# A fixed TensorE order in the mixing stage, and state products in 64-column form

## The chip, the cores and the metric

The kernel runs on one core of a Trainium2 chip. The metric is the device time of one execution in microseconds. Three runs of the kernel before took 3265.79, 3265.83 and 3274.77 us, median 3265.83. One more execution was profiled; it took 3262.19 us, and all rows below are from it.

## The reference, cut to what matters

One layer of a decoder on 2,048 tokens of 1,024 channels, in float32. Half of the channels go through an RWKV-7 recurrence, half through dilated attention; the mixture is projected and normalised, then follow a mixture of 32 experts, a gated embedding and a second normalisation.

```python
proj = h @ w_in                                  # r,k,v for 8 rwkv heads, q,k,v for 8 attention heads
# rwkv, per head, over the tokens (state is 64 x 64):
sa    = state @ a_t
state = state * w_t + outer(sa, b_t) + outer(v_t, k_t)
y_t   = state @ r_t
# attention: three patterns (window, step) = (128,1), (512,4), (2048,16), each with a bias and a softmax,
# then one softmax over the three log-sums weighs the three results
x = layer_norm(ALPHA * x + concat(y_rwkv, y_att) @ w_o)
x = layer_norm(ALPHA * x + experts(x) + sigmoid(x @ G) * (p @ P))
```

## The kernel before, in words

The kernel runs its stages one after the other: project (inputs to r, k, v, q and what the recurrence needs), mixers (recurrence and attention), mix_out (normalising the recurrence's heads, product with w_o, first normalisation, router), ple, experts, finish. The change is in mixers, from about 860 to 1800 us of the profile.

The recurrence is worked in chunks of 128 tokens. The eight heads form four pairs u, and a pair lies on the 128 partitions, one head on 64. For a pair and two chunks (q = 0 to 7, c = 0, 1) three generators do the work. rwkv_front (L652) makes triangular products (triangles, L650), sends their diagonal blocks through DRAM twice, inverts them on VectorE (L691, L692) and leaves U. rwkv_inverse (L706) turns U into the inverse of the whole triangle with ten small products and copies, and ends with WF (L800). rwkv_state (L803) makes the products that belong to a chunk (L822 to L865: RB, MK, MJ, E, Q, the transposed v in vt) and then goes from chunk to chunk (L867 to L890). This last loop has the two products of the change:

- the next state. pn is MK x vt plus E x st over the whole 128 by 128 (L875, L877), though a state has only the two diagonal blocks of 64 by 64, one for each head. MK and E hold both heads, and of pn only the diagonal blocks are read: ScalarE scales the upper one (L880), VectorE the lower one (L882), into the other of two state tiles. The blocks off the diagonal of a state tile stay at the zeros that L527 wrote.
- the output. py is vt x MJ for each head on its own 64 rows (L886), plus st x Q as one product over 128 rows (L888). ScalarE copies it out (L890).

In the first chunk there is no st, in the last no next state: 60 new states and 64 outputs over four pairs and 16 chunks.

attn_streams (L975) gives three streams that share the blocks of attention, 16 to a pass, 12 passes. A block is logits (L1066 or L1069), bias and minimum (L1079, L1082), exponential (L1085), transposes (L1091), a copy (L1095, L1097) and the product with the values (L1105), copied out by VectorE (L1117 to L1121). When the three patterns of two heads are done, combine (L1131, L1140) weighs them by way of DRAM (L1213, L1160).

All these are generators. Before each piece of work they yield an engine and a cost, such as _pe(448) or _act(64). weave (L117) is the planner: plain code that keeps one clock for each engine and picks among the streams the one that can start first, with 100 ns between two steps of a stream (LATENCY, L65), and among those within SLACK of it the one first in the list, states first. The order of the picks is the order of the program text. The Tile framework then orders the instructions of each engine by a time model of its own, so that an instruction whose operands are not there in that model is passed by others. Where a with block calls manual_schedule for an engine, that engine's instructions keep the order of the text. project (L219), mix_out (L1420) and the stages after it have such blocks for TensorE; mixers has none.

Of the kernel before, what the change touches and what calls it, by code (L numbers as in the profile page):

```python
# [12 lines left out]
AF = mybir.ActivationFunctionType  # L13
# [5 lines left out]
P = 128  # L19
# [43 lines left out]
FRONTS = 2  # L63
# [55 lines left out]
def _act(n):  # L119
    return "ACT", 190 + 0.56 * n  # L120


def _dve(n):
    return "DVE", 60 + 1.06 * n
# [6 lines left out]
def _pe(ns):  # L131
    return "PE", ns


def _wait(ns):
    return "DMA", ns
# [31 lines left out]
class K:  # L168
# [634 lines left out]
    def rwkv_state(self, i, u, q, pp):  # L803

        nc, kp = self.nc, self.rk_
        mm = nc.tensor.matmul
        ps = lambda: self.rps[i].tile([P, BT], F32, name=f"ps{i}", tag=f"ps{i}")
        T = lambda name, shape, bufs=1: kp.tile(shape, F32, name=f"{name}{i}", tag=f"{name}{i}", bufs=bufs)
        RB = T("RB", [P, 2, 2, 192])
        H = [slice(0, 64), slice(64, 128)]  # L810
        col = [slice(c * P, (c + 1) * P) for c in range(2)]
        while "v" not in pp:
            yield None
        rt, v = ([pp[m][:, cs] for cs in col] for m in ("rt", "v"))
        bk = [pp["bk"][:, c] for c in range(2)]
        MJ, MK = T("MJ", [P, 2, 2, P]), T("MK", [P, 2, P])
        yield _pe(950)
        prs = [ps().rearrange("p (c k s) -> p c k s", c=2, k=2) for _ in range(2)]
        for c in range(2):
            for m in range(2):  # L820
                for h in range(2):
                    mm(prs[h][:, c, m], bk[c][H[h], m], rt[c][H[h]], start=True, stop=True)  # L822
        for h, pr in enumerate(prs):
            yield _dve(2 * P)
            nc.vector.tensor_tensor(out=RB[:, h, :, 0:P], in0=pr[:, :, 0, :], in1=self.c("upi").unsqueeze(1).to_broadcast([P, 2, P]), op=ALU.mult)
            yield _dve(2 * P)
            nc.vector.tensor_tensor(out=MJ[:, h], in0=pr[:, :, 1, :], in1=self.c("upi").unsqueeze(1).to_broadcast([P, 2, P]), op=ALU.mult)
        vt = T("vt", [P, 2, P])
        for m in range(2):
            yield _pe(430 - 215 * m)  # L830
            pt = ps().rearrange("p (k s) -> p k s", s=P)
            for j in range(2 - m):
                for c in range(2):
                    nc.tensor.transpose(pt[:, 2 * j + c], v[c] if m else bk[c][:, j], self.c("eye"))
            yield _act((4 - 2 * m) * P)
            if m:
                nc.scalar.copy(vt, pt[:, 0:2])
            else:
                nc.scalar.copy(RB[:, :, :, P:192], pt[:, 0:2].rearrange("p c (h k) -> p h c k", h=2))
                nc.scalar.copy(MK, pt[:, 2:4])  # L840
        while "WF" not in pp:
            yield None
        WF = pp["WF"]
        pm = []
        for h in range(2):
            yield _pe(660)
            pm.append(ps()[:, 0:384].rearrange("p (c s) -> p c s", s=192))
            for c in range(2):
                mm(pm[h][:, c], WF[:, h, c, 64:192], RB[:, h, c], start=True, stop=True)
        for h in range(2):  # L850
            yield _dve(384)
            nc.vector.tensor_tensor(out=MJ[:, h], in0=pm[h][:, :, 0:P], in1=MJ[:, h], op=ALU.add)
            nc.vector.tensor_tensor(out=MK[:, :, H[h]], in0=pm[h][:, :, P:192], in1=MK[:, :, H[h]], op=ALU.add)
        yield _pe(700)
        pq = ps()[:, 0:384].rearrange("p (c s) -> p c s", s=192)
        for c in range(2):
            for h in range(2):
                mm(pq[H[h], c], WF[:, h, c, 0:64], RB[:, h, c], start=True, stop=True)
        yield _dve(256)
        E = self.E[i]  # L860
        for h in range(2):
            nc.vector.tensor_tensor(out=E[H[h], :, H[h]], in0=pq[H[h], :, P:192], in1=self.c("eye2")[H[h]].unsqueeze(1).to_broadcast([64, 2, 64]), op=ALU.add)
        yield _dve(256)
        Q = T("Q", [P, 2, P])
        nc.vector.tensor_tensor(out=Q, in0=pq[:, :, 0:P], in1=pp["rt"].rearrange("p (c s) -> p c s", s=P), op=ALU.add)  # L865
        yt = T("yt", [P, 2 * P])
        for c in range(2):  # L867
            first = q == 0 and c == 0
            last = q == 7 and c == 1
            st, after = (self.state[u][(c + n) % 2] for n in range(2))  # L870
            if not last:
                yield _pe(224 if first else 448)
                pn = ps()[:, 0:P]

                mm(pn, MK[:, c], vt[:, c], start=True, stop=first)  # L875
                if not first:
                    mm(pn, E[:, c], st, start=False, stop=True)  # L877
                yield _act(64)
                rho = self.rho[:, u, q + c, 1 - c:2 - c]
                nc.scalar.activation(after[H[0], H[0]], pn[H[0], H[0]], AF.Copy, scale=rho[H[0]])  # L880
                yield _dve(64)
                nc.vector.tensor_scalar_mul(after[H[1], H[1]], pn[H[1], H[1]], rho[H[1]])  # L882
            yield _pe(640)
            py = ps()[:, 0:P]
            for h in range(2):
                mm(py[H[h]], vt[:, c, H[h]], MJ[:, h, c], start=True, stop=first)  # L886
            if not first:
                mm(py, st, Q[:, c], start=False, stop=True)  # L888
            yield _act(128)
            nc.scalar.copy(yt[:, col[c]], py)  # L890
        nc.sync.dma_start(self.y[u * P:(u + 1) * P, q * 2 * P:(q + 1) * 2 * P], yt)
        pp["done"] = True

    def mixers(self, attention=True):

        self.y = self.scratch("y", (D, S))
        rounds = [(q, u) for q in range(8) for u in (0, 2)]
        pps = [[{}, {}] for _ in rounds]

        def load(n):  # L900
            q, u = rounds[n]
            for i in range(2):
                self.rwkv_load(u + i, q, pps[n][i])

        begun = {}

        def fronts(s):
            for n in range(s, len(rounds), FRONTS):
                if n in begun:
                    yield from begun[n]  # L910
                    continue
                while n >= ROUNDS and not all("done" in pp for pp in pps[n - ROUNDS]):
                    yield None
                load(n)
                yield _wait(2500)
                yield from self.rwkv_front(n, pps[n], pps[n - 1])

        def inverses(i):
            for n in range(len(rounds)):
                yield from self.rwkv_inverse(i, pps[n][i])  # L920

        def states(i):
            for n, (q, u) in enumerate(rounds):
                yield from self.rwkv_state(i, u + i, q, pps[n][i])
                self.steps[0] += 1

        with ExitStack() as es:
            att = []
            self.rwkv_setup(es)
            self.busy = False  # L930

            with self.tc.high_priority():
                for n in range(FRONTS):
                    load(n)
                    begun[n] = self.rwkv_front(n, pps[n], pps[n - 1])
                    while next(begun[n], None) is not None:
                        pass
            if attention:
                self.attn_open(es)
                att = self.attn_streams()  # L940
            self.steps = [0, 0]

            def late():

                return range(4 + FRONTS, 8 + FRONTS) if self.steps[1] < (self.steps[0] + HEAD) * PACE else (4 + FRONTS,)

            weave([states(0), states(1), inverses(0), inverses(1), *(fronts(s) for s in range(FRONTS)), *att], late)


    def attn_bias(self, tile, bank):  # L950
# [1042 lines left out]
```

## Time and profile before

| | before |
|---|---|
| median of 3 runs | 3265.83 us |
| profiled execution | 3262.19 us |
| its span | 3260.4 us |
| TensorE (PE) busy | 2938.1 us, 90% |
| VectorE (DVE) busy | 2118.0 us, 65% |
| ScalarE (ACT) busy | 1529.3 us, 47% |
| GpSimd (POOL) busy | 675.4 us, 21% |
| mean granted TensorE clock | 0.934 |

PE is the matmuls, PEld the weight loads that run beside them. A row's form is partitions*columns of the stationary operand, then the moving one. A matmul's row lasts until its result is out, longer than the time to the next one's start, so work is counted from start to start. "<-" names what an engine waited for.

### The profile page before, as it was taken

The page shows a single profiled execution, that of the slowest core. Times are in us where ns is not written, and L with a number is a line of the kernel's source. Part 1 is how long each engine was busy: PE and PEld are TensorE (multiplying, and loading weights), DVE is VectorE, ACT ScalarE, POOL GpSimd, SP SyncE. Part 2 cuts the span into 40 slices and gives each one's busy share as a digit, 9 for nine tenths or more (in the row PEclk, how much of TensorE's full clock was granted, in tenths as well). Part 3 has the DMA queues.
Part 4 walks back from the last instruction along what each step waited for, and adds up shares of the span by engine and source line. Part 5 has one row for each costly group of instructions (what it writes and reads, how often), then busy time and mean ns, then how long its engine had stood idle before and what let it go on. Part 6 is the DMA issues. An engine that isn't in the chain of part 4 may idle for free. (4 is left out here: it accounts for less than half of the span.)

```text
span 3260.4 us, 49197 instructions
## 1 busy us (share of the span) xinstructions
PE 2938.1 (90%) x16686; PEld 2343.0 (72%) x16687; DVE 2118.0 (65%) x4730; ACT 1529.3 (47%) x3650; POOL 675.4 (21%) x682
## 2 busy tenths in 40 slices
PE   7989888999798999998998799899999999998880
PEld 6666777777676777777786577788777777776660
DVE  4997333786654766655757688653577777766756
ACT  3434212554444544543543333311477777765642
POOL 0442000344100211111202122223011111112216
PEclk9999999999898988998897999999999999999985
DMA  5213433788615335234214453243599999987846
GB/s 172 74 59 99 107 81 80 215 273 267 139 55 127 94 74 129 72 95 104 75 31 130 144 183 123 97 138 89 181 298 322 326 301 324 315 296 220 293 129 209
DMA packets 364061, 533.04 MB, mean 163 GB/s; under 512 B 92376, under 2 KB 204640, under 8 KB 363792
## 3 DMA queue, kind: packets, MB, share of 16 engines
q1 hardware_dynamic: 330144, 459.09, 44.1%
q0 software_dynamic: 14496, 45.93, 6.0%
q10 hardware_dynamic: 19168, 24.86, 3.1%
q8 instruction: 133, 2.18, 0.3%
q14 instruction: 120, 0.98, 0.1%
HBM read 402.27 MB, written 128.06 MB: 163 GB/s over the span
## 5 line engine op out<-in xcount | busy, mean ns | idle before, releaser
L1708 DVE TENSOR_TENSOR wl<-raw,wh 128x512 fp32r<-128x512 f32 x768 | 478.3, 681 | 88.4 <-ACT wh L1707 87.7
L1707 ACT CAST wh<-raw 128x512 fp32r<-128x512 f32 x768 | 417.3, 620 | 13.2 <-DMA raw<-in_w_up_dram 12.1
L198 PE MATMUL ps<-xh,wh 128*128 128x512 f32 x640 | 262.6, 410 | 1.1 <-ACT xh L322 1.0
L199 PE MATMUL ps<-xl,wh 128*128 128x512 f32 x640 | 258.7, 404 | 1.2 <-DVE xl L323 1.2
L200 PE MATMUL ps<-xh,wl 128*128 128x512 f32 x640 | 258.2, 403 | 0.0
L1085 ACT ACTIVATE pe<-pe,ms 128x256 f32<-128x256 f32 (+1 forms) x384 | 174.8, 457 | 144.0 <-DVE ms L1082 133.0
L1837 POOL DMA_INDIRECT acc<-ysb,ix x48 | 95.8, 1996 | 623.0 <-ACT ysb L1836 403.0
L198 PE MATMUL pe<-wh,XX 128*128 128x512 f32 x480 | 199.8, 416 | 3.8 <-ACT wh L1707 3.8
L199 PE MATMUL pe<-wl,XX 128*128 128x512 f32 x480 | 192.0, 400 | 2.6 <-DVE wl L1708 2.6
L200 PE MATMUL pe<-wh,XX 128*128 128x512 f32 x480 | 190.9, 398 | 0.0
L198 PEld LDWEIGHTS ps<-xh,wh 128*128 128x128 f32 x640 | 124.7, 195 | 34.6 <-issue 2.6
L199 PEld LDWEIGHTS ps<-xl,wh 128*128 128x128 f32 x640 | 124.7, 195 | 30.1 <-DVE xl L323 2.4
L200 PEld LDWEIGHTS ps<-xh,wl 128*128 128x128 f32 x640 | 124.1, 194 | 29.5
L1091 PE MATMUL pl<-eye,pe 128*128 128x128 f32 x600 | 126.3, 299 | 10.7 <-ACT pe L1085 9.6
L1066 PE MATMUL pl<-KK,Q 128*128 128x256 f32 x432 | 115.4, 393 | 15.6 <-DMA KK<-ks 8.0
L198 PE MATMUL pb<-gh,XH 128*128 128x512 f32 x320 | 126.1, 394 | 0.0
L199 PE MATMUL pb<-gl,XH 128*128 128x512 f32 x320 | 125.2, 391 | 0.0
L1752 PE MATMUL pe<-wh,XX 128*128 128x512 f32 x288 | 120.1, 417 | 5.4 <-ACT wh L1707 5.4
L200 PE MATMUL pb<-gh,XL 128*128 128x512 f32 x320 | 124.9, 390 | 0.0
L1105 PE MATMUL po<-pe,V 128*64 128x128 f32 x1200 | 119.4, 300 | 3.6 <-DVE O L1117 3.2
L1753 PE MATMUL pe<-wl,XX 128*128 128x512 f32 x288 | 118.8, 413 | 2.9 <-DVE wl L1708 2.9
L1082 DVE CUSTOM_DVE_ANT_0 pe<-pl,bias 128x256 f32<-128x256 f32 x216 | 82.6, 418 | 59.7 <-PE pl L1066 37.4
(418 smaller groups left out, 7627.5 us busy)
## 6 DMA issues: line engine op xcount, KB each, us to landing
raw<-in_w_gate_dram SPq DMA_DIRECT2D x128, 512.0 KB
raw<-in_w_up_dram SPq DMA_DIRECT2D x128, 512.0 KB
raw<-in_w_down_dram SPq DMA_DIRECT2D x128, 512.0 KB
pk<-pk SPq DMA_DIRECT2D x32, 512.0 KB
pk_t<-pk SPq DMA_DIRECT2D x32, 512.0 KB
KK<-ks SPq DMA_DIRECT2D x64, 256.0 KB
wr<-in_w_in_dram SPq DMA_DIRECT2D x48, 256.0 KB
rkk<-rkk SPq DMA_DIRECT2D x32, 384.0 KB
```

Source lines behind the costliest of these rows:

```text
L198: mm(out, lh, rh, start=first, stop=False)
L199: mm(out, lh, rl, start=False, stop=False)
L200: mm(out, ll, rh, start=False, stop=last)
L1066: mm(pl[:, h], q, toks(KK[:, m, h], n, prev, 2), start=m == 0, stop=m == 1)
L1085: nc.scalar.activation(pe[:, h, w], pe[:, h, w], AF.Exp, bias=m_[h], scale=-1.0, accum_out=s_[h])
L1091: nc.tensor.transpose(pt[:, h, b], pe[:, h, b * P:(b + 1) * P], self.c("eye"))
L1105: mm(o[h * 64:(h + 1) * 64, j], vb[:, h * 64:(h + 1) * 64], tt[:, h, b], start=b == kb[0], stop=b == 1)
L1707: nc.scalar.copy(wh[:, c], raw[:, c])
L1708: nc.vector.tensor_tensor(out=wl[:, c], in0=raw[:, c], in1=wh.bitcast(F32)[:, c], op=ALU.subtract)
L1752: mm(ps, L[:, 0:P], wh, start=first, stop=False)
L1753: mm(ps, L[:, 0:P], wl, start=False, stop=last)
L1837: nc.gpsimd.indirect_dma_start(out=self.acc, out_offset=bass.IndirectOffsetOnAxis(ap=ix[0:r, e, b:b + 1], axis=0), in_=ysb[0:r], in_offset ...
```

## The change

In rwkv_state each product is made for the two heads apart, with 64 columns of the stationary operand each: pn shrinks to 64 columns and holds one head's state in each half of the partitions; the output's product with the state is two half products. The costs that are told to the planner are changed. In mixers, the call of weave stands in a manual_schedule block for TensorE.

```diff
             if not last:
-                yield _pe(224 if first else 448)
-                pn = ps()[:, 0:P]
-
-                mm(pn, MK[:, c], vt[:, c], start=True, stop=first)
+                yield _pe(110 if first else 220)
+                pn = ps()[:, 0:64]
+
+                for h in range(2):
+                    mm(pn[H[h]], MK[:, c, H[h]], vt[:, c, H[h]], start=True, stop=first)
                 if not first:
-                    mm(pn, E[:, c], st, start=False, stop=True)
+                    for h in range(2):
+                        mm(pn[H[h]], E[:, c, H[h]], st[:, H[h]], start=False, stop=True)
                 yield _act(64)
                 rho = self.rho[:, u, q + c, 1 - c:2 - c]
-                nc.scalar.activation(after[H[0], H[0]], pn[H[0], H[0]], AF.Copy, scale=rho[H[0]])
+                nc.scalar.activation(after[H[0], H[0]], pn[H[0]], AF.Copy, scale=rho[H[0]])
                 yield _dve(64)
-                nc.vector.tensor_scalar_mul(after[H[1], H[1]], pn[H[1], H[1]], rho[H[1]])
-            yield _pe(640)
+                nc.vector.tensor_scalar_mul(after[H[1], H[1]], pn[H[1]], rho[H[1]])
+            yield _pe(220 if first else 440)
             py = ps()[:, 0:P]
             for h in range(2):
                 mm(py[H[h]], vt[:, c, H[h]], MJ[:, h, c], start=True, stop=first)
             if not first:
-                mm(py, st, Q[:, c], start=False, stop=True)
+                for h in range(2):
+                    mm(py[H[h]], st[:, H[h]], Q[:, c], start=False, stop=True)
...
-            weave([states(0), states(1), inverses(0), inverses(1), *(fronts(s) for s in range(FRONTS)), *att], late)
+            with self.tc.manual_schedule(engines={mybir.EngineType.PE}):
+                weave([states(0), states(1), inverses(0), inverses(1), *(fronts(s) for s in range(FRONTS)), *att], late)
```

## Rows read from the trace of the kernel before

**Rows 1.** The page: busy time of the engines, and TensorE's granted clock in 40 slices

```profile
PE 2938.1 (90%) x16686; PEld 2343.0 (72%) x16687; DVE 2118.0 (65%) x4730; ACT 1529.3 (47%) x3650; POOL 675.4 (21%) x682
PEclk9999999999898988998897999999999999999985
```

**Rows 2.** Busy time by stretch; the columns stand in its first line

```profile
core 0: us, PE busy (x) PEld busy (x) DVE busy (x) ACT busy (x) POOL busy (x), PEclk, DMA share, GB/s
900.00:1800.00 900.00, 848.73 (x6702) 684.86 (x6701) 552.25 (x1929) 422.39 (x1426) 142.24 (x215) 0.91 0.36 90
1700.00:1800.00 100.00, 85.55 (x612) 68.96 (x608) 71.21 (x154) 38.13 (x96) 26.95 (x24) 0.78 0.43 113
1717.60:1815.00 97.40, 72.34 (x430) 56.66 (x428) 65.78 (x138) 32.91 (x79) 23.64 (x15) 0.72 0.56 158
```

**Rows 3.** TensorE's waits, 900 to 1800 us: us in total, times, longest

```profile
PE ps L858 <- DVE AW L721: 14.6, 2, 9.2
PE ps L877 <- DVE E L862: 8.6, 3, 7.4
PE pl L1066 <- DMA KK<-ks: 7.3, 4, 3.0
```

**Rows 4.** TensorE's timeline, one chunk: start us, us, engine, line, tiles, form, count

```profile
1445.61 0.71 PE L1091 MATMUL pl<-eye,pe 128*128 128x128 f32 x5
1446.15 0.39 PE L875 MATMUL ps<-vt,MK 128*128 128x128 f32 x2
1446.38 0.39 PE L877 MATMUL ps<-S,E 128*128 128x128 f32 x2
1446.69 0.44 PE L886 MATMUL ps<-MJ,vt 128*64 128x128 f32 x4
1447.06 0.49 PE L888 MATMUL ps<-Q,S 128*128 128x128 f32 x2
1447.48 0.71 PE L858 MATMUL ps<-RB,WF 128*64 128x192 f32 x6
```

**Rows 5.** TensorE's timeline, 1309 to 1311.4 us, products and one weight load

```profile
1308.98 0.60 PE L834 MATMUL ps<-eye,pk_t 128*128 128x128 f32 x4
1309.51 0.68 PE L788 MATMUL ps<-t,X 64*64 64x64 f32 x8
1310.12 0.33 PE L1091 MATMUL pl<-eye,pe 128*128 128x128 f32 x1
1310.29 0.60 PE L834 MATMUL ps<-eye,pk_t 128*128 128x128 f32 x4
1310.82 0.66 PE L1105 MATMUL po<-pe,V 128*64 128x128 f32 x8
1311.40 0.44 PE L834 MATMUL ps<-eye,v_t 128*128 128x128 f32 x2
...
1310.81 0.42 PEld L1105 LDWEIGHTS po<-pe,V 128*64 128x64 f32 x8 [0.17 <-issue]
```

**Rows 6.** Groups by line, 900 to 1800 us: busy us, mean ns, idle before

```profile
L1085 ACT ACTIVATE pe<-pe,ms 128x256 f32<-128x256 f32 (+1 forms) x341 | 154.7, 455 | 122.7 <-DVE ms L1082 114.5 <-PE ps L650 2.9 <-DMA KK<-ks 2.5
L1082 DVE CUSTOM_DVE_ANT_0 pe<-pl,bias 128x256 f32<-128x256 f32 x186 | 71.2, 419 | 58.3 <-PE pl L1066 36.5 <-PE po L1105 20.1 <-ACT vt L837 1.1
L1085 ACT ACTIVATION_READ_ACCUMULATOR pe<-pe,ms 128x1 f32 x341 | 64.6, 189 | 0.0
...
L875 PE MATMUL ps<-vt,MK 128*128 128x128 f32 x120 | 27.5, 313 | 0.7 <-ACT AW L728 0.4 <-DVE MK L853 0.3
```

**Rows 7.** Timelines at the stage's end

```profile
1714.70 0.59 PE L756 MATMUL ps<-U,AB 32*32 32x32 f32 x16
1715.22 0.44 PE L834 MATMUL ps<-eye,v_t 128*128 128x128 f32 x2
1716.97 0.66 PE L1105 MATMUL po<-pe,V 128*64 128x128 f32 x8 [0.28 <-ACT pe L1095]
...
1742.16 1.27 POOL L1213 TENSOR_TENSOR O<-O,O 128x512 f32<-128x512 f32 x1 [8.52 <-DMA O<-fac]
...
1748.10 0.69 DVE L1160 TENSOR_TENSOR O<-O,O 128x512 f32<-128x512 f32 x1
...
1798.00 0.47 PE L888 MATMUL ps<-Q,S 128*128 128x128 f32 x2
1810.08 0.80 PE L198 MATMUL pa<-woh,YH 128*128 128x512 f32 x1 [8.38 <-ACT YH L1335]
```

## The prediction

> **What bounds the kernel now.** I read four views in this order: the page's shares and slices, the busy time by stretches, the waits of TensorE, and the timeline of TensorE in the mixing stage. The page says that TensorE (PE) is busy for 90% of the span, VectorE (DVE) for 65% [rows 1]. The change touches only the mixing stage. Between 900 and 1800 us, nearly all of that stage, PE is busy for 848.7 of 900 us and DVE for 552.3 [rows 2], so PE bounds the stage: work taken from PE shortens it, and so does each wait at the head of its queue that goes. The waits add up to 900 - 848.7 = 51.3 us; the largest are 14.6 us for DVE before L858 and 8.6 us for DVE before L877 [rows 3].
>
> The timeline shows what PE's time is made of. A float32 product stands there as two passes (L875 has 120 rows [rows 6] for 60 products). Full-array passes of 128 columns follow each other at 0.11 us: L834 and L1091 do so, and so do L875 and L877 [rows 4, 5]. Three things matter for the change.
> - Half-array passes (128*64), issued for the two column halves, run side by side: eight L1105 passes take 1310.82 to 1311.40, 0.58 us [rows 5], that is four pairs of 0.11 and 0.14 besides.
> - That rest is the price of a change of array shape. L834's four passes take 0.53 us before a 64*64 product follows, where 4 x 0.11 = 0.44 would do [rows 5]: 0.09 to leave a shape. Entering costs about 0.05 more (0.14 - 0.09).
> - 64*64 passes of 64 columns on one quadrant come at (1310.12 - 1309.51 - 0.14)/8 = 0.06 us [rows 5].
>
> Going through this timeline from 900 to 1800 us, I count 939 places where a matmul has another array shape than the one before it; rows 4 and 5 hold some of them.
>
> At the stage's end the last attention product runs at 1716.97, the last state product at 1798.00, and the next stage only gets going after a wait of 8.4 us before 1810.08 [rows 7]. Of the 97.4 us from 1717.6 to 1815 PE is busy for 72.3, at a granted clock of 0.72 [rows 2]. That is a mean of the two levels, 2.4 and 1.2 GHz; PE had been waiting there for one chain after the other.
>
> **Part 1, the state products in 64 columns.** New state (L875, L877): four full passes of 128 columns, 4 x 0.11 = 0.448 us, become eight half-array passes of 64 columns. If the two halves run side by side as L1105's do, that is four pairs of 0.058, 0.23 us: 0.216 us saved in each of 56 products and half of that in the 4 first ones, 12.5 us. No row shows a 128*64 pass with 64 columns, so the bounds: not side by side, 8 x 0.058 = 0.46, 1 us lost; at the spacing of the smallest passes, L756's sixteen in 0.52 us [rows 7], four pairs of 0.032, about 18 us saved. I take 12.5, since the nearest row (L1105) shows pairs.
>
> Output (L886, L888): two pairs and two full passes, 0.22 + 0.22 = 0.44, become four pairs, 0.44: nothing. The measured stretch is longer, L886 at 1446.69 to L858 at 1447.48, 0.79 against L1105's 0.58 [rows 4, 5], because the shape changes inside it. That change goes, but the new state, now half-array as well, gets one at its own border. The planner's list (below) has 797 changes with the old shapes and 799 with the new, so this is no gain of its own. The copies L880 and L882 read 64 columns before and after: nothing. What the smaller products free is PE's own time; late next is the same ACT or DVE copy.
>
> The Trainium skill ("TensorE: Matmul & The Clock Gate", section "The mechanism") speaks against this part: it says that a weight load overlaps a running matmul only where the row groups differ, and both halves use all 128 rows here. This trace disagrees: L1105's eight weight loads lie within 0.42 us, under matmuls that take 0.66 [rows 5]. What the rule would give here is worked out as the last rival.
>
> **Part 2, PE's order.** The planner (weave) is plain host code that goes by its own costs. Written out for the kernel before, it makes 1,262 PE steps. In that order the array shape changes 797 times, because a step's products stay together; in the trace, steps are cut up and mixed (L834 stands twice with L788 and L1091 between [rows 5]). With 139 changes fewer at 0.14 us: 19.5 us. Bounds: 0, if the new costs reorder the steps into as many changes, and 28, if each costs 0.2 as on entering the full array (L888's two passes take 1447.06 to 1447.48, 0.42 for 0.22 of work [rows 4]).
>
> **Part 3, waits.** From now on a step whose operand is late holds all of PE. Behind a late state product stand attention's logits, transposes and value products of three streams, and behind those DVE (L1082) and ACT (L1085, L1095), which have nothing else to do for these streams. Today's order was settled instruction by instruction, with work passing by whatever was not ready: it runs attention up to some 650 matmuls ahead of the planner's order and leaves the state products to the end. How far the planner can be trusted: it counts 0.48 us for an exponential of 256 columns, the rows show 0.455 and 0.189 for its sum, 0.64 together [rows 6]; 0.33 for L1082, the row shows 0.419 [rows 6]. It is also too short for PE: 596 us in all where the stage's PE is busy for about 850 [rows 2]. Both sides stretch by about 1.3 to 1.4, so what it put between two dependent steps still roughly covers their hand-over. Bounds for the waits: down to 14 us, which leaves of 51.3 only what lies after 1700 us (85.6 of 100 busy [rows 2]); up to 110, about twice today's, or one more wait of 0.05 us at each of 1,262 steps. By the planner's own clock PE idles 9.5% until its last state product, which on this stage's 817 us of work left (848.7 less 32) would be 86 us. I take 62, the middle of the two bounds, 11 more than now.
>
> SP's and POOL's queues are not edited, but what they wait for comes in another order: loads of keys and of rwkv operands are issued when PE has read the old ones. Their rows are short today, 7.3 us for L1066 behind the key loads [rows 3]; they are inside the bounds above.
>
> **Part 4, the end.** In the planner's list the last state product is step 1,186, and the 76 after it are attention's. So the end turns round: today the rwkv chain is last, and of the 97.4 us after 1717.6 some 45 are lost (72.3 busy at a clock of 0.72 are 52 us of work at the full one [rows 2]). Afterwards attention is last, then its weighting: 25 us from the last product to the first multiplication (1716.97 to 1742.16 [rows 7]), 6 more to the first finished slice (L1160 at 1748.10), 12 until a result is back in the next stage, as today from the last state product to the first unbroken run (1798.00 to 1810.08 [rows 7]): 43, and a little where three streams are alone. I take no difference, with 25 us either way.
>
> **The sum.** -12.5 (part 1) - 19.5 (part 2) + 11 (part 3) + 0 (part 4) = -21 us. The profiled execution took 3262.2 us (span 3260.4 and 1.8 around it), which gives 3241. The median of the runs shown is 3265.8, 3.6 above it; on that scale, which the times below use too, 3245.
>
> **The rivals.**
> - A, the order is better than I allow. Waits fall to 14 us: -12.5 - 19.5 - 37 = -69, 3197. For it: PE has much parallel work, and the state chain, late today, would be in step. Against it: PE already has only 5.7% idle.
> - B, slower: PE blocks at the head of its queue. The mechanism is part 3's, all along the stage, where a state or inverse step waits for DVE (L862, L853, L750) with attention behind it. It decides once the waits exceed 51 + 32 = 83 us. At 110 us, with the clock's half level a little more often (a mean of 0.90 for 0.91 [rows 2], 10 us), it is -32 + 59 + 10 = +37: 3303. For it: DVE is 61% busy in the stage [rows 2], the planner's hand-overs of 0.1 us and costs are short, and its own idle share gives 86. Against it: PE's own steps stretch as much.
> - C, no difference. The new passes don't pair, and the order brings as many waits as it saves changes: +1 - 19.5 + 20 = about 0, 3266.
> - D, slower: the halves' weight loads wait for the running passes. Eight loads of 0.053 (L1105's 0.42 [rows 5]) and eight passes of 0.058 are 0.89 for a new state (+0.44); with passes of 0.11 they are 1.30 for an output (+0.51 on 0.79); over 60 products +57 us, with the rest of the sum (-19.5 + 11) 3314. L1105 stands against it. It is the rule named in part 1 that would make it so.
>
> **Chances.** Forecast 0.46, A 0.12, B 0.27, C 0.12, D 0.03. A measurement of this kernel can tell about 0.3%, 10 us, from nothing. The forecast's own range is 3220 to 3262, most of it faster by more than 10 us (0.40), a little within (0.06). With A this gives faster 0.52; same is 0.12 and 0.06, 0.18; slower 0.30. The range over all cases, from A's time to short of B's farther end, is 3200 to 3305.
>
> **What would show it.** The row of L875 with 240 passes of 64 columns and pairs 0.06 us apart: part 1; at 0.11 a pair, it brings nothing. Fewer than 850 changes of shape between 900 us and the stage's end: part 2. PE's idle time in the stage: 62 us for the forecast, over 83 for B. The last attention product after the last state product: part 4. The prediction is wrong if the stage's end moves by more than 45 us, or if time moves in stages after it that the change leaves alone.

## The result and the profile after

The kernel after takes 3381.67 us (median of 4 runs, 3377.93 to 3387.09); the kernel before took 3265.81 beside it. The ratio is 1.0351, 95% interval 1.0328 to 1.0374: slower by 3.5%, where 0.6% faster was forecast, and outside the forecast range. The profiled execution took 3378.72 us, 116.5 more than that of before.

All of it lies in the mixing stage. The first product of the next stage's output bank (pn at L1322, now L1326) starts at 1931.47 us instead of 1815.06, 116.4 later. The change moves all later line numbers: by 1 to 3 in the state loop, by 4 in the attention and the next stage (L1105 is L1109).

The page after, first its busy times, then the granted clock of the 40 slices:

```profile
PE 2895.4 (86%) x17038; PEld 2294.3 (68%) x17039; DVE 2119.1 (63%) x4730; ACT 1535.3 (45%) x3650; POOL 671.3 (20%) x682
PEclk9999999898898799889896599999999999999895
```

PE works 42.7 us less than in [rows 1] and the kernel takes 116 us longer. The clock has a new hole at slices 22 and 23 (1773 to 1942 us), the end of the stage. Busy time of the kernel after by stretches, cut at the last state product and at the first pn:

```profile
core 0: us, PE busy (x) PEld busy (x) DVE busy (x) ACT busy (x) POOL busy (x), PEclk, DMA share, GB/s
864.00:1772.50 908.50, 776.44 (x7137) 624.47 (x7137) 530.42 (x1906) 409.35 (x1379) 131.67 (x223) 0.90 0.33 79
1772.50:1931.50 159.00, 76.57 (x338) 49.91 (x333) 63.94 (x185) 51.98 (x155) 18.13 (x12) 0.57 0.37 102
900.00:1800.00 900.00, 764.27 (x6921) 610.25 (x6921) 512.76 (x1845) 399.22 (x1357) 125.61 (x208) 0.89 0.34 83
```

The stretch of the kernel before that answers to the first row; its counterpart to the second is the last of [rows 2], cut a tenth later there, at 72.38 busy:

```profile
864.00:1717.60 853.60, 814.85 (x6600) 658.28 (x6600) 520.80 (x1931) 415.33 (x1436) 125.78 (x211) 0.93 0.34 84
```

This gives the ledger. Before: 814.85 + 72.38 = 887.2 us busy and 38.8 + 25.1 = 63.9 idle. After: 776.44 + 76.57 = 853.0 busy and 132.1 + 82.4 = 214.5 idle. So PE is busy 34.2 us less, close to the 32 of parts 1 and 2, and stands idle 150.6 us longer: 93.3 up to the first cut, 57.3 behind it. The clock was lower with it: from 864 us to the first pn PE's clock stood at 1.2 GHz for 327 us, before for 181, and 212 us of PE's busy time lie in that, before 156.

TensorE's waits after, 864 to 1960 us (us in total, times, longest), which answer to [rows 3]:

```profile
PE pa L1326 <- DMA y<-y: 46.4, 1, 46.4
PE po L1109 <- DVE O L1121: 23.6, 10, 10.9
PE ps L650 <- DVE MK L853: 22.3, 17, 12.7
PE pl L1095 <- ACT pe L1089: 22.1, 31, 2.2
PE ps L650 <- DVE mn L1164: 11.9, 1, 11.9
```

None of these was among the large ones before. Many more are short: up to the first cut 96 waits of 0.15 to 1 us add up to 48 us, before 15 of them to 6 us. L650 (the triangles) reads only what was loaded from DRAM, neither MK nor mn. What it waits for is the PSUM bank it writes. Each side of the recurrence owns two banks (the pools rps), the two generators of a side and, on side 0, the fronts take them in turn, and L853 is the addition on DVE that frees one. L1109 waits in the same way for L1121 to copy out the attention's bank.

One of the long ones in the timeline after:

```profile
1342.42 1.26 POOL L703 TENSOR_TENSOR U<-ct,Vc 128x512 f32<-128x512 f32 x1 [7.92 <-PE ps L797]
...
1342.85 0.48 PE L650 MATMUL ps<-pk_t 64*128 64x128 f32 x2
1344.07 2.71 SPq L1157 DMA_DIRECT2D stat<-ms  x2
...
1352.68 0.37 SPq L1161 DMA_DIRECT2D stt<-stat  x1
...
1355.19 0.19 DVE L1164 TENSOR_TENSOR mn<-stt 128x32 f32<-128x32 f32 x1 [15.93 <-DMA stt<-stat]
...
1355.63 0.28 DVE L853 TENSOR_TENSOR MK<-ps,MK 128x128 f32<-128x128 f32 x1
...
1356.06 1.19 PE L650 MATMUL ps<-pk_t 64*128 64x128 f32 x6 [12.73 <-DVE MK L853]
```

Read from below: PE's triangles wait 12.7 us for a bank, the bank for L853, and L853 stands on DVE behind L1164, which waits for the attention's statistics on their way through DRAM. For most of that time no engine works. DVE has such waits at its head in the kernel before too (34.1 us for stt, 41.8 after). But there 24 us of PE's gaps coincide with DVE's waits of over 1 us at L1160, and after 38 us with those at L1164. These long waits are thus some 14 us of the growth and not most of it.

The end of the stage after, which answers to [rows 7]:

```profile
1859.09 1.12 PE L1109 MATMUL po<-pe,V 128*64 128x128 f32 x8 [0.73 <-ACT pe L1099]
...
1880.68 1.26 POOL L1217 TENSOR_TENSOR O<-O,O 128x512 f32<-128x512 f32 x1 [1.69 <-DMA O<-fac]
...
1898.89 4.67 SPq L1221 DMA_DIRECT2D y<-O  x2
...
1903.60 0.43 SPq L1317 DMA_DIRECT2D y<-y  x1
...
1906.94 1.19 PE L1326 MATMUL pa<-y,ct 128*128 128x256 f32 x2 [46.38 <-DMA y<-y]
...
1931.47 1.05 PE L1326 MATMUL pn<-y,ct 128*128 128x256 f32 x2
```

From the last state product at 1772.5 to 1860 us, the value products of 26 attention blocks run with nothing of the recurrence beside them, 63 of 88 us busy. Then their weighting runs alone, and the next stage's first load (L1317) is issued on SP only behind all of the weighting's transfers, 44 us after the last attention product. What it loads are rows of the recurrence, whose last product ended at 1772.8, so by the code it waits for its place in the queue and not for its data; no run tested that.

### The profile page after: what moved, and what is told of

It reads as the page before. It is cut to its first block, busy times and chain, and to the rows that moved or that the text cites. A ratio compares the mean times of both kernels' runs of the same rounds, so it can differ in the third digit from the quotient of the medians.

```text
span 3376.8 us, 49753 instructions
## 1 busy us (share of the span) xinstructions
PE 2895.4 (86%) x17038; PEld 2294.3 (68%) x17039; DVE 2119.1 (63%) x4730; ACT 1535.3 (45%) x3650; POOL 671.3 (20%) x682
## 3 DMA queue, kind: packets, MB, share of 16 engines
q1 hardware_dynamic: 330144, 459.09, 42.7%
## 5 line engine op out<-in xcount | busy, mean ns | idle before, releaser
L198 PE MATMUL ps<-xh,wh 128*128 128x512 f32 x640 | 262.9, 411 | 0.0
L198 PE MATMUL pe<-wh,XX 128*128 128x512 f32 x480 | 198.8, 414 | 4.2 <-ACT wh L1711 4.2
L1109 PE MATMUL po<-pe,V 128*64 128x128 f32 x1200 | 123.7, 324 | 49.9 <-DVE O L1121 23.6
L198 PEld LDWEIGHTS ps<-xh,wh 128*128 128x128 f32 x640 | 124.4, 194 | 33.6 <-issue 2.8
L1095 PE MATMUL pl<-eye,pe 128*128 128x128 f32 x600 | 117.9, 310 | 23.8 <-ACT pe L1089 22.1
L1109 PEld LDWEIGHTS po<-pe,V 128*64 128x64 f32 x1200 | 73.2, 155 | 84.0 <-DVE O L1121 23.7
L198 PE MATMUL pb<-gh,XH 128*128 128x512 f32 x320 | 126.5, 395 | 0.0
```

What stands on the lines that cost most here:

```text
L198: mm(out, lh, rh, start=first, stop=False)
L1095: nc.tensor.transpose(pt[:, h, b], pe[:, h, b * P:(b + 1) * P], self.c("eye"))
L1109: mm(o[h * 64:(h + 1) * 64, j], vb[:, h * 64:(h + 1) * 64], tt[:, h, b], start=b == kb[0], stop=b == 1)
```

## The experiments

Each ratio is to runs of the kernel before on the same chip (medians there 3265.8 to 3275.2 us). In the texts below "theory B" is that of the banks, which I formed after the result; it is not the forecast's rival B.

**1. Which half of the change costs.** e1 is the kernel after without the line that fixes the order; e2 has the products and costs of before with that line.

```
e1:  -            with self.tc.manual_schedule(engines={mybir.EngineType.PE}):
e2:  +            with self.tc.manual_schedule(engines={mybir.EngineType.PE}):
```

> The state products in 64-column form with the planner's new costs, PE's order left to the time model as before. Theory W (the loss is made by the fixed order: waits at the head of PE's queue all along the stage, and attention last at its end): 12.5 us of passes go, 3250 us (3240 to 3262). Rival F (the half-array products themselves are dear, weight loads or shape changes): over 3290 us.

Measured: 3252.03 us, 0.9924 (0.9905 to 0.9943).

> The fixed order alone, with the old products and their old costs. W: the whole loss stays and the passes' 12.5 us are missing on top, 3394 us (3380 to 3410), PE's idle time up to the last state product again 120 us or more. F: near 3265 us.

Measured: 3386.52 us, 1.034 (1.0323 to 1.0358). The order makes the whole loss. The new products in the time model's order gain 0.8%, and under the fixed order they gain nothing that can be measured (1.0351 with them).

**2. The end and the hand-overs.** HEAD is the lead in steps that the weave (the planner) gives attention, LATENCY the ns that it leaves after each step before the next of its stream.

```
e3:  -HEAD = 10          +HEAD = 22
e4:  as e3, and  -LATENCY = 100.0    +LATENCY = 300.0
```

> The changed kernel with the planner's HEAD at 22 instead of 10: attention is hurried until it is 22 state steps ahead, so that in the planner's list the last attention step comes 93 steps before the last state step (in the changed kernel 76 steps after it). W: the turned end goes back, about 60 us of idle time and half clock saved, the waits along the stage stay: 3320 us (3300 to 3335). Rival E (the end is the whole loss): 3265 us or less. If the waits along the stage are all of it: 3375 to 3385.

Measured: 3342.57 us, 1.0223 (1.0205 to 1.0241), above the expected range. Attention now ends first (last product 1773.5, last state product 1897.8). HEAD = 22 was worth 39 us here, 1.3 percentage points. It does more than turn the end back: the next stage now starts 65 us ahead of the last state product, at

```profile
1832.86 0.70 PE L1326 MATMUL pa<-y,ct 128*128 128x256 f32 x2 [0.80 <-DMA y<-y]
```

and 28 us of its products lie before that point. In the kernel before it started 17 us ahead, in the kernel after 47 us behind the last attention product. They come behind the weave in the text, some of them (L198) from a manual_schedule block of their own, so the order of the text is kept within a block and not between two. HEAD also moves attention's steps all along the stage, so the 39 us are not the end's alone.

> As with HEAD 22, and the planner counts 300 ns between two steps of a stream instead of 100, nearer to what a hand-over takes (the planner leaves out the drain of a matmul and the read of an accumulator). W with waits from too short a planned hand-over: a third to a half of the waits go, 3285 us (3270 to 3305). If the waits come from something that the planner does not know (DMA, slots, the order of DVE and ACT): as with HEAD 22 alone, within 10 us, or slower.

Measured: 3306.94 us, 1.01 (1.0085 to 1.0116), 36 us off and just above the range for short hand-overs. PE's idle time up to the stage's last product did not fall (156 us in e3, 159 in e4; all gaps counted). PE's busy time did, from 877.6 to 850.1 us, with 205 us of it at 1.2 GHz against 240. The waits for banks grew; the row of e3 and then that of e4, 864 to 1960 us:

```profile
PE ps L650 <- DVE MK L853: 22.0, 17, 7.7
```

```profile
PE ps L650 <- DVE MK L853: 43.9, 25, 13.3
```

**3. Banks, whose order, and a planner that counts banks.** e5 makes one pool of four of the two pools of two. e6 and e6b hold only one mixer to the weave's order. e7 and e12 let the weave count banks.

```
e5:  as e3, and
-        self.rps = [pool(f"rps{n}", 2, space=PSUM) for n in range(2)]
+        self.rps = [pool("rps", 4, space=PSUM)] * 2      # and one tag, "ps", for all their tiles
e6:  as e3, but manual_schedule is entered only around next() of streams i < 4 + FRONTS
e6b: as e3, but only around those of streams i >= 4 + FRONTS (attention)
e7:  -HEAD = 10               +HEAD = 18
     +    def take(self, i, n):              # ahead of each step that takes banks of side i
     +        while self.held[i] + n > 2:
     +            yield None
     +        self.held[i] += n              # held is lowered at the copy that frees a bank
```

> The kernel after with HEAD = 22 (3342.6 us alone), and the two PSUM pools of two banks (one for each half of the RWKV streams) made one pool of four. Theory B (banks): the matmul queue stands at its head for a PSUM bank of its own pool (62 us in the trace with HEAD = 22: the waits of L650, L834 and the like for DVE and ACT copies) while the other pool has one free; with four to choose from most of these waits end earlier, and the slot waits fall to 30 us or less: 3300 to 3320 us. Rival I (interplay: what stands at the head waits for its data or for the other mixer, whatever the banks): the waits change their name only, 3335 to 3350 us.

Measured: 3308.39 us, 1.0108 (1.0072 to 1.0145). The time is as theory B has it, and L650's wait for MK falls from 22.0 to:

```profile
PE ps L650 <- DVE MK L853: 5.2, 4, 3.3
```

But other waits grew (L1109 for L1099 from 8.9 to 19.7 us), and PE's idle time in sum hardly fell. Up to the last state product, e3 and then e5 (columns as above):

```profile
864.00:1897.80 1033.80, 877.57 (x7520) 703.22 (x7522) 604.69 (x2086) 461.12 (x1536) 151.98 (x238) 0.86 0.33 83
864.00:1865.10 1001.10, 848.20 (x7514) 682.19 (x7512) 602.57 (x2103) 459.16 (x1536) 151.65 (x236) 0.88 0.34 85
```

That is 156.2 us idle against 152.9, and 877.6 us busy against 848.2; 240 and then 198 us of the busy time stood at 1.2 GHz. So four common banks bring 34 us, but that they bring it by less waiting is not shown: the waits changed their names, as rival I has it, and PE worked at a higher clock.

> HEAD = 22, and only the RWKV streams are held to the weave's order on TensorE; the attention's matmuls are placed by the time model again. If the loss is in how the weave orders the six RWKV streams among themselves (banks, theory B): stays near 3330 us. If it is in how attention and RWKV are laid into one another (rival I): 3255 to 3275 us.

Measured: 3294.63 us, 1.0064 (1.0043 to 1.0085).

> The mirror of the run before: only the attention's matmuls are held to the weave's order, the RWKV streams are placed by the time model, HEAD = 22. Theory B: 3255 to 3275 us. Rival I: 3255 to 3275 us as well; if the attention's own order is at fault: near 3330 us. The two mirrors together tell whose order costs.

Measured: 3250.82 us, 0.9917 (0.9884 to 0.995). Attention in the weave's order costs nothing beside e1. The recurrence in the weave's order (e6) costs 1.5 points against e6b, though less than both together (e3). e6 lies between its two ranges, so neither expectation fits whole: the order of the recurrence is at fault, and attention held to that order makes it worse.

> The whole stage in the weave's order as in the kernel after, but the weave now counts the two PSUM banks of each RWKV side and the one WF buffer, and gives a stream its step only when a bank is free; HEAD = 18 (the last attention matmul then stands 120 RWKV passes before the last state pass, so that the end of the stage is like that with HEAD = 22). Theory B: the slot waits fall from 62 us to 25 or less and nothing else grows as much: 3285 to 3310 us. Rival I: the waits move to data and to the attention, 3335 to 3355 us.

Measured: 3434.14 us, 1.0488 (1.0449 to 1.0527), a miss. The wait that replaced the others, in e7's trace:

```profile
PE ps L755 <- POOL U L711: 134.1, 7, 48.9
```

U comes from the fronts. A front needs both banks of side 0 at once, and with my count it got them only when nobody else held one. That is a flaw of this experiment, so it was repeated as e12. (e7 and e12 also let the weave count the one WF buffer of a side.)

**4. Repeats, controls and the sum.** e8 joins the three edits that helped, e9 puts the four banks beside the time model's order, and in e11 the weave counts 5 us for a DMA.

```
e8:  e5 with  -LATENCY = 100.0   +LATENCY = 300.0
e9:  e1 with the pool of e5
e11: e3 with  -yield _wait(2500)   +yield _wait(5000)     (eight places)
e12: e7 with HEAD = 22; a waiting front is served before the others of side 0
```

> The kernel after with three edits together: HEAD = 22, one pool of four PSUM banks, LATENCY = 300. Alone on HEAD = 22 the banks took 34 us off (3342.6 to 3308.4) and LATENCY 36 us (to 3306.9). If they are separate causes, the terms add: 3268 to 3280 us, that is the time of the kernel before. If both only loosen the same waits: 3295 to 3310 us.

Measured: 3239.11 us, 0.99 (0.9852 to 0.9947): 69 us under e5, about twice what LATENCY gave beside the two pools, and below both expected ranges. With three edits the fixed order is now 1% faster than the kernel before. That is no more than e1 has without it (0.9924); the intervals overlap.

> The control for the banks: the 64-column forms in the time model's order (3252.0 us) with one pool of four banks. If banks bind only where TensorE's order is fixed (the time model lays other work over a taken bank): 3242 to 3260 us, no gain. If four common banks are worth the same anywhere: 3215 to 3230 us.

Measured: 3245.11 us, 0.9933 (0.9905 to 0.996): no gain over e1. Four common banks help only where the order is fixed.

> HEAD = 22 (3342.6 us), and each of the weave's eight estimates of a DMA in the mixing stage 5000 ns instead of 2500. If the weave lays products too early because it thinks that what comes over DRAM (the small inverses, the attention's statistics) is back sooner than it is: 3305 to 3325 us. If what it misses is banks and the copies out of them: 3335 to 3350 us.

Measured: 3341.21 us, 1.0217 (1.0168 to 1.0265): nothing. The weave's DMA estimates are not the cause.

> The weave counts banks as in the run e7_plan_banks (3434.1 us), but a front that waits for two banks is served before the other streams of its side, and HEAD = 22. In that run TensorE stood 134 us for U, which comes from the fronts. If the fronts were starved there by my accounting: the wait for U falls under 20 us and the time to 3300 to 3325 us (theory B as it should have been tried). If a plan with few banks is slow in itself: above 3380 us.

Measured: 3323.05 us, 1.0147 (1.0098 to 1.0197). The wait for U is gone, and 0.8 points of e3's loss are. A plan that knows the two banks recovers part of it; whether four banks (e5) recover more the intervals do not tell.

**5. What was still open.**

```
e13: e8 with the products and costs of the kernel before
e14: e8 with  -HEAD = 22         +HEAD = 10
e15: e8 with  -LATENCY = 300.0   +LATENCY = 500.0
```

> The products and costs of the kernel before, with the fixed order mended by the three edits (HEAD = 22, four common banks, LATENCY = 300); with the 64-column forms the same is 3239.1 us. If TensorE's work sets the time once its waits are mended, the forms' gain of part 1 of the forecast (12.5 us) shows here as a loss: 3248 to 3262 us. If the waits still set it: 3234 to 3244 us.

Measured: 3235.77 us, 0.9895 (0.9842 to 0.9947): no loss without the 64-column products. Busy time to the stage's last product, e8 and then e13 (columns as above):

```profile
864.00:1791.80 927.80, 804.48 (x7466) 659.04 (x7464) 585.31 (x2089) 449.16 (x1530) 148.33 (x225) 0.90 0.36 91
```

```profile
864.00:1789.10 925.10, 815.22 (x7139) 669.45 (x7140) 603.88 (x2107) 452.90 (x1543) 149.63 (x227) 0.91 0.36 92
```

With the new products PE works 10.7 us less (804.5 against 815.2) and stands 13.4 us longer (123.3 against 109.9). Some 2 us of the 10.7 are not theirs, as 17.6 us of the next stage's products lie in the first row and 19.5 in the second. Their gain has become idle time; the costs told to the weave differ too, so part of the longer idle time may come from another order.

> The run e8_banks_lat300 (3239.1 us) with HEAD = 10 as in the kernel after: the attention's last blocks (206 of its matmuls) stand behind the last state pass again. If the turned end costs what it did beside the two pools and LATENCY = 100 (3381.7 to 3342.6 us): 3272 to 3285 us. If the shorter way to the last state step pays for it: 3235 to 3250 us.

Measured: 3298.92 us, 1.0083 (1.0058 to 1.0108). HEAD = 10 costs 60 us here, more than the range had. The row of its trace that the kernel after has as well:

```profile
PE pa L1326 <- DMA y<-y: 46.7, 1, 46.7
```

> The run e8_banks_lat300 with LATENCY = 500. If the distance between a product and its use is still too short at 300: 3215 to 3232 us. If banks or the chain of states bind now: 3238 to 3265 us.

Measured: 3235.26 us, 0.99 (0.9844 to 0.9955), the same as with 300 and between the two ranges.

## Why the prediction was wrong, by its steps

**Part 1, right for PE and worthless for the time under the fixed order.** The groups by line of the kernel after, 900 to 1800 us (answering to L875 in [rows 6]):

```profile
L876 PE MATMUL ps<-vt,MK 128*64 128x64 f32 x240 | 20.1, 249 | 5.9 <-DVE AW L721 4.5 <-DVE AB L668 0.6 <-DVE S L884 0.5
...
L879 PE MATMUL ps<-S,E 128*64 128x64 f32 x224 | 17.4, 234 | 0.5 <-DVE E L862 0.5
```

and one chunk of its timeline:

```profile
1200.07 0.20 PEld L876 LDWEIGHTS ps<-vt,MK 128*64 128x64 f32 x4 [0.17 <-PE pl L1095]
1200.07 0.34 PE L876 MATMUL ps<-vt,MK 128*64 128x64 f32 x4
1200.18 0.20 PEld L879 LDWEIGHTS ps<-S,E 128*64 128x64 f32 x4
1200.24 0.29 PE L879 MATMUL ps<-S,E 128*64 128x64 f32 x4
...
1201.95 0.44 PE L888 MATMUL ps<-MJ,vt 128*64 128x128 f32 x4
...
1202.22 0.39 PE L891 MATMUL ps<-Q,S 128*64 128x128 f32 x4
```

A new state's eight passes take 1200.07 to 1200.53. From start to start of the next matmul, less the idle time before that one, its lines now take 23.7 us, before 35.0: 11.3 saved, 12.5 forecast. The output, put at nothing, saved as much: its two lines take 38.8 us, before 51.4 (864 us to the stage's end). In the time model's order the new products with their costs were worth 21 us (e1). The halves' loads ran under the matmuls, which ends rival D. The Trainium skill ("TensorE: Matmul & The Clock Gate", section "The mechanism") allows a load to overlap a running matmul only where the row groups differ. Here both halves use all rows and four loads stand within 0.20 us beside four passes of 0.34, so this trace disagrees again with that rule; what the same section says of loads into a background weight buffer, that they go ahead of running matmuls, would fit it. "Late next is the same ACT or DVE copy" was the sentence to follow up: in e13 the saving stands as idle time.

**Part 2, right in the count, its price not shown.** From 864 us to the stage's last product the array shape changes 974 times before and 803 after, 171 fewer. The forecast's 139 set 900 to 1800 us of the trace against the planner's whole list; like against like would have been 974 - 799 = 175. With part 1 the forecast was 32 us less work, and the ledger has 34.2, but made of other terms (last section). e13, with 760 changes and the old products, is 1% faster than the kernel before; how much of that the changes make was not separated.

**Part 3, the step that failed first.** I forecast 11 us more waiting, with 110 us in all as the outer bound. The idle time up to the cut went from 38.8 to 132.1, by 93 us; between 900 and 1800 us it is 135.7, where 62 was forecast. My reason was that PE's steps and the hand-overs stretch by the same 1.3 to 1.4, so that the weave's distances would hold. It left out that the weave knows nothing of PSUM banks. A step that has its data and no bank holds the whole queue, and this is a wait between streams that no stretching of a stream covers. That the number of banks costs time under the fixed order, and only there, e5 (34 us), e12 and the control e9 show; the row of L650 names the wait. The Trainium skill ("Perfetto Trace Analysis", section "Matmuls") has the general rule, that independent groups of matmuls should rotate through different banks so that copying one out overlaps the next group; the kernel does so with two a side. In the time model's order two were enough, as e9 shows, and in the fixed one they were not. The second cause is the distance itself. LATENCY = 300 brings 36 us beside the two pools and 69 with four banks, so the two pools had hidden half of it. How banks and distance come to cost time stays open in part: in e4 and e5 PE's idle time is about that of e3, and its busy time is 27 and 29 us shorter, with 35 and 42 us less of it at 1.2 GHz. Why the clock stood higher with as much idle time was not taken apart, nor why the weave's 100 ns is too little: it may be queueing on DVE and ACT, whose order is still the time model's, as in the timeline at 1343 us. PE and DVE both in the weave's order, and LATENCY = 300 without the fixed order, were not tried.

**Part 4, the second step that failed.** "No difference, 25 us either way" was measured as 39 us (e3) and 60 us (e14), with what else HEAD moves; the idle time behind the cut grew by 57.3. The sum of 43 us for attention, weighting and next stage left out two things. "A little where three streams are alone" was 88 us for 63 of work, much of it at the 1.2 GHz level, as the granted clock of 0.57 from 1772.5 to 1931.5 says. And I took the first finished slice for the start of the next stage, while its loads are issued on SP's queue behind every transfer of the weighting, 44 us after the last attention product against the 31 that I had counted to the first slice. The queue past which this work is moved, SP's, was left to a bound of part 3. Nor did it see that a recurrence that ends last lets the next stage's products run beside it, as in e3.

**Rivals.** B had the sign, the mechanism and the point from which it decides (83 us of waits; there are 132 idle up to the cut). Its price of 37 us was too small, since its 110 us were no real bound, and it held nothing for the end. With 0.30 on slower I had weighed what spoke for B, the weave's own 86 us of idle time, too low. A and C fell. The ladder of e3, e5 and e8 (1.0351, 1.0223, 1.0108, 0.99) takes the loss back in three steps: attention's lead with the end, the banks, the distance between dependent steps. The 1% below the kernel before is about what the products gain without the order (e1) and the mended order without the products (e13): the two gains do not add up.

## What to carry to other kernels

A fixed order on one engine is only as good as what its planner counts. Before fixing one, list what the planner does not know (banks, buffers, the order on the engines that copy out) and ask of each step what queues behind it if that is missing. Ask also which stream ends last and what the next stage then waits for, down to the queue that issues its loads. And work taken from an engine that waits for copies can show up as idle time, so read a saving against the idle time of its stage, not against the engine's busy share.

## What was not expected of the hardware

Products of 64 rows on the two row halves profit much from alternating between the halves. L822 has the same 480 passes in 900 to 1800 us in both kernels; the row of before and then that of after:

```profile
L822 PE MATMUL ps<-pk_t 64*128 64x128 f32 x480 | 69.8, 308 | 0.0
```

```profile
L822 PE MATMUL ps<-pk_t 64*128 64x128 f32 x480 | 38.3, 290 | 0.9 <-ACT yt L893 0.8
```

Nothing of L822 was edited. The program text alternates the halves. The time model parted them: before, more than half of the passes stand in runs of eight, by the code those of one half, 0.11 us apart. In the fixed order sixteen stand together, and in the steady part of such a run the second pass of a pair starts 7 ns after the first. One step of each kernel:

```profile
1100.98 1.16 PE L822 MATMUL ps<-pk_t 64*128 64x128 f32 x8
1102.06 0.33 PE L1091 MATMUL pl<-eye,pe 128*128 128x128 f32 x1
1102.32 1.16 PE L822 MATMUL ps<-pk_t 64*128 64x128 f32 x8
```

```profile
1117.28 1.45 PE L822 MATMUL ps<-pk_t 64*128 64x128 f32 x16
```

From start to start of the next matmul, less the idle time before that one, the line takes 36.6 us instead of 64.9; e1, in the time model's order, has 58.1, e13, in the fixed one with the old products, 34.7. With L650, which has the same form, it is 86.8 instead of 128.6 us from 864 us to the first pn: 42 us, more than the ledger's whole 34.2. No part of the forecast had this as a term of its own. That PE's busy time still met the forecast is chance: with the time at 1.2 GHz counted as half, its work fell by some 62 us (an estimate from 156 and 212 us busy at that level), and the lower clock took 28 of them back.
